# The B and C parameters of an S5 layer, loaded in pairs onto 128 partitions

## The chip, the cores and the metric

One core of a Trainium2 chip runs the whole model as one program. The metric is the time of the program on the device in microseconds (us). The kernel before took 1530.77 us in the median of 3 runs (1530.55 to 1533.98). The profiled execution took 1534.4 us, of which 1532.5 us are the profile's span.

The engines named here: PE does the matrix products, DVE and ACT the elementwise work, POOL some small things, SP issues nearly all DMA transfers, in its own program order. Each engine runs its instructions strictly in the order in which they were written.

## The reference, cut to what matters

Two layers work on 256 latent and 256 context tokens of width 2048, all in float32. Layer 0 multiplies the modulated input with a matrix of 2048x6144; beside attention heads it has a bidirectional S5 state-space group, whose parameters are discretized first:

```
h  = x  * (1 + sc) + sh          # sc, sh, gt = split(silu(c) @ ada_w + ada_b)
u  = h @ w_in[:, 4096:5120]      # 64 groups of 16 channels
lb = exp(a * dt);  f = (lb - 1) / a;  bb = f * b      # complex, 2 directions x 64 groups x 64 states (x 16)
state[t] = lb * state[t-1] + bb @ u[t];   y[t] = Re(c @ state[t])
```

`s5_b_re`, `s5_b_im`, `s5_c_re` and `s5_c_im` are the four arrays that this case is about: each has 2 x 64 x 1024 float32 values, 512 KB.

## The kernel before

**The stage.** The change lies in the first stage, which ends about 196 us after the span's start. Three streams meet in it on PE.

- The modulation. `ada_blocks` multiplies silu(c) with the first 4096 columns of `ada_w`: 8 blocks of 256 columns, 4 pieces each, so 32 groups of 8 matmuls `a<-adp,cst`. I count them from 1 to 32. Each group needs a pair of DMA loads into a tile `adp` (two times 512 KB); there are three such tiles (AHEAD = 3), so the load for group n+3 is issued only when group n is done. 33.6 MB come in this way.
- The modulated input. `h_blocks` transposes the tokens (`sb<-ident,xs`), block by block, and ACT and DVE make the two-part form `big_h`, `big_l`.
- The main products. `first` multiplies each block of the input with 11 (blocks 1 to 5) or 8 (blocks 6 to 8) column tiles of `w_in`. A float32 product is made of three passes (high times high, high times low, low times high), so the stage has 158 triples of `128x512` matmuls, 474 matmuls. The weights come as tiles `raw` of 384 to 512 KB, which ACT and DVE split into `hi` and `lo`.

**The S5 parameters.** `s5_params` is a generator that runs in the background of the same stage, from block 2 on. It loads each of the four arrays into a tile `nat` with the 64 groups on partitions 0 to 63 (line 764), and there is one such tile only. B is turned by 2 x 8 transposes per array, C by 2 x 16 small matmuls with the identity (both `sb<-ident,nat`), and ACT copies the result from the bank into the tile `cc`. Between B and C stand the powers of the discretized step (`cpow`, on DVE, into `pw`), the two copies of them into `pd_t` (ACT), and the six products of 128x1024 that make `bbar` from B (DVE). B's products use the tile `nat` as scratch (`tb`). C takes B's place in `cc`, and so comes after the last product.

**What sets the order.** Before the program is built, Python code (`Clock`) keeps an estimated time for every engine and for the DMA queue. After each triple of main matmuls `pump` asks which background generators are due by these estimates, and lets them write their next instructions. So every change of an instruction's estimated time, a load's above all, can move all that is written after it on every engine. On the chip nothing of these estimates is left but the order: PE waits at a group whose load has not landed, even if main products further down are ready.

Of the kernel before, what the change touches and what calls it, by code (L numbers as in the profile page):

```python
# [23 lines left out]
F32 = mybir.dt.float32  # L24
# [6 lines left out]
P = 128  # L31
# [10 lines left out]
G = 64  # L42
# [7 lines left out]
def dram(t, offset, ap):  # L50
    return bass.AP(tensor=t.tensor, offset=t.offset + offset, ap=ap)
# [197 lines left out]
def backbone(ctx: ExitStack, tc: tile.TileContext, A, out):  # L249
    nc = tc.nc  # L250
    clock = Clock()
    V, S, PE = Timed(nc.vector, "dve", clock), Timed(nc.scalar, "act", clock), Timed(nc.tensor, "pe", clock)
    GP, SY = Timed(nc.gpsimd, "gp", clock), Timed(nc.sync, "sp", clock)
# [3 lines left out]
    def pool(stack, name, bufs, **kw):  # L257
        pools.append(Pool(stack.enter_context(tc.tile_pool(name=name, bufs=bufs, **kw)), clock, bufs))
        return pools[-1]
# [20 lines left out]
    def hbank():  # L280
        return sbs[0].tile([P, 512], F32, name="sb")

    def vacant():

        while sbs[0].free("sb") > clock.now() + 0.05:
            clock.ready = sbs[0].free("sb") - pace["margin"]
            yield
# [7 lines left out]
    def act(o, i, f=AF.Copy, **kw):  # L295
        return S.activation(o, i, f, **kw)


    ident = const.tile([P, P], F32, name="ident")
# [183 lines left out]
    def aform(t0, n, nk=KT, k0=0):  # L483

        ps = mbank()
        for k in range(nk):
            if k % 8 == 0:
                wh, wl = ws.get()
            mm3(ps[:, :n], wh[:, k % 8, :], wl[:, k % 8, :], big_h[:, k0 + k, t0:t0 + n], big_l[:, k0 + k, t0:t0 + n],
                k == 0, k == nk - 1)  # L490
            used[0] = k
            pump()
        return ps
# [253 lines left out]
    def s5_params(sp, pp):  # L747
        tl, ts, ar, ai = (T5[n] for n in ("tl", "ts", "ar", "ai"))
        l8 = sp.tile([P, 2, 2, G], F32, name="l8")
        pd_t = sp.tile([P, 8, 2, G], F32, name="pd_t")  # L750
        bbar = sp.tile([P, 2, G + 1, 16], F32, name="bbar")
        cc = sp.tile([P, 2, G, 16], F32, name="cc")
        dcol = sp.tile([32, G], F32, name="dcol")
        zk = sp.tile([32, 16], F32, name="zk")
        T5.update(l8=l8, pd_t=pd_t, bbar=bbar, cc=cc, dcol=dcol, zk=zk)
        dn = pp.tile([G, 16], F32, name="dn")
        SY.dma_start(dn, dram(A["s5_d"], 0, [[16, G], [1, 16]]))
        bre, bim = cc[:, 0], cc[:, 1]
        dst = {"s5_b_re": bre, "s5_b_im": bim, "s5_c_re": cc[:, 0], "s5_c_im": cc[:, 1]}
        nat = {}  # L760

        def load_nat(nm):
            t = pp.tile([P, 2048], F32, name="nat")[:G]
            SY.dma_start(t.rearrange("g (k n) -> g k n", k=2),
                         dram(A[nm], 0, [[1024, G], [G * 1024, 2], [1, 1024]]))
            nat[nm] = t

        def params(nm):
            t = nat.pop(nm)
            for c8 in range(2):  # L770
                yield from vacant()
                p = hbank()
                for c_ in range(8):
                    c = c8 * 8 + c_
                    o = p[:, c_ * G:(c_ + 1) * G]
                    if "_b_" in nm:
                        PE.transpose(o, t[:, c::16], ident[:G, :G])
                    else:
                        for k in range(2):
                            PE.matmul(o[64 * k:64 * k + 64], t[:, k * 1024 + c * 64:k * 1024 + c * 64 + 64],  # L780
                                      ident[:G, :G], start=True, stop=True)
                act(dst[nm][:, :, c8 * 8:c8 * 8 + 8], p.rearrange("p (c g) -> p g c", c=8),
                    scale=-1.0 if nm == "s5_c_im" else 1.0)
                yield

        load_nat("s5_b_re")
        yield
        yield from vacant()
        pa = hbank()
        PE.transpose(pa[:16, :G], dn, ident[:G, :G])  # L790
        V.memset(dcol, 0.0)
        V.tensor_copy(dcol[:16], pa[:16, :G])
        V.memset(zk, 0.0)
        V.tensor_copy(zk[:16], ident[:16, :16])
        V.memset(bbar[:, :, G], 0.0)
        yield
        yield from params("s5_b_re")
        load_nat("s5_b_im")
        yield
        yield from params("s5_b_im")  # L800
        pw = pp.tile([P, 9, 2, G], F32, name="pw")
        V.memset(pw[:, 0, 0], 1.0)
        V.memset(pw[:, 0, 1], 0.0)
        V.tensor_mul(pw[:, 1, 0], tl("mag"), tl("cn"))
        V.tensor_mul(pw[:, 1, 1], tl("mag"), tl("sn"))
        den, nr, f = tl("t0"), tl("t1"), pp.tile([P, 2, G], F32, name="f")
        V.tensor_mul(den, ar, ar)
        V.tensor_mul(tl("t2"), ai, ai)
        V.tensor_add(den, den, tl("t2"))
        V.reciprocal(den, den)  # L810
        ni = pw[:, 1, 1]
        ts(nr, pw[:, 1, 0], -1.0, None, OP.add)
        V.tensor_mul(f[:, 0], nr, ar)
        V.tensor_mul(tl("t2"), ni, ai)
        V.tensor_add(f[:, 0], f[:, 0], tl("t2"))
        yield "dve"
        V.tensor_mul(f[:, 1], ni, ar)
        V.tensor_mul(tl("t2"), nr, ai)
        V.tensor_sub(f[:, 1], f[:, 1], tl("t2"))
        for s in range(2):  # L820
            V.tensor_mul(f[:, s], f[:, s], den)
        yield
        tp4 = pp.tile([P, 4, G], F32, name="tp4")

        def cpow(lo, cnt, by):

            s0 = lo - by
            xr, xi = pw[:, s0:s0 + cnt, 0], pw[:, s0:s0 + cnt, 1]
            yr = pw[:, by, 0][:, None, :].to_broadcast([P, cnt, G])
            yi = pw[:, by, 1][:, None, :].to_broadcast([P, cnt, G])  # L830
            t = tp4[:, :cnt]
            V.tensor_mul(pw[:, lo:lo + cnt, 0], xr, yr)
            V.tensor_mul(t, xi, yi)
            V.tensor_sub(pw[:, lo:lo + cnt, 0], pw[:, lo:lo + cnt, 0], t)
            V.tensor_mul(pw[:, lo:lo + cnt, 1], xr, yi)
            V.tensor_mul(t, xi, yr)
            V.tensor_add(pw[:, lo:lo + cnt, 1], pw[:, lo:lo + cnt, 1], t)

        cpow(2, 1, 1)
        yield "dve"  # L840
        cpow(3, 2, 2)
        yield "dve"
        cpow(5, 4, 4)
        yield "dve"
        for s in range(2):
            V.tensor_copy(l8[:, 0, s], pw[:, 8, 0])
        ts(l8[:, 1, 0], pw[:, 8, 1], -1.0, None)
        V.tensor_copy(l8[:, 1, 1], pw[:, 8, 1])
        act(pd_t[:64], pw[:64, 7::-1])
        act(pd_t[64:], pw[64:, :8])  # L850
        yield
        fr = f[:, 0, :, None].to_broadcast([P, G, 16])
        fi = f[:, 1, :, None].to_broadcast([P, G, 16])
        tb = pp.tile([P, 2048], F32, name="nat")[:, :1024].rearrange("p (g c) -> p g c", c=16)
        V.tensor_mul(bbar[:, 0, :G], bre, fr)
        yield "dve"
        V.tensor_mul(tb, bim, fi)
        yield "dve"
        V.tensor_sub(bbar[:, 0, :G], bbar[:, 0, :G], tb)
        yield "dve"  # L860
        V.tensor_mul(bbar[:, 1, :G], bim, fr)
        yield "dve"
        V.tensor_mul(tb, bre, fi)
        yield "dve"
        V.tensor_add(bbar[:, 1, :G], bbar[:, 1, :G], tb)
        load_nat("s5_c_re")
        yield
        yield from params("s5_c_re")
        load_nat("s5_c_im")
        yield  # L870
        yield from params("s5_c_im")
        yield

# [197 lines left out]
    pp = pool(pp5, name="pp5", bufs=1)  # L1071
# [304 lines left out]
    def hilo(o, ps, n=512, bufs=1):  # L1376
        h = att.tile([P, 512], F32R, name=o + "h", bufs=bufs)
        l = att.tile([P, 512], F32R, name=o + "l", bufs=bufs)
        act(h[:, :n], ps)
        V.tensor_sub(l[:, :n], ps, h[:, :n])  # L1380
        return h, l
# [113 lines left out]
    for h in range(NAH):  # L1495
# [13 lines left out]
        k = hilo("k", aform(0, NT))  # L1509
# [132 lines left out]
    t, st_ = layer0_half(1)  # L1642
# [75 lines left out]
    for hf in range(2):  # L1718
# [3 lines left out]
        for n in range(4):  # L1722
# [4 lines left out]
            else:  # L1727
                o = slice((n - 2) * 256, (n - 1) * 256)
# [71 lines left out]
    for hp in range(8):  # L1800
# [3 lines left out]
        r = rms(qx.rearrange("p t h d -> p (t h) d"))  # L1804
# [23 lines left out]
    with ExitStack() as es:  # L1828
# [5 lines left out]
        t = fp.tile([P, 2, D], F32, name="t1")  # L1834
        st_ = fp.tile([P, 2, 8, 6], F32, name="st1")
        mv = fp.tile([P, 2, 2], F32, name="mv1")
        nm = fp.tile([P, 1], F32, name="nm")
# [43 lines left out]
        for i in range(2):  # L1881
# [19 lines left out]
            if i == 1:  # L1901
                V.scalar_tensor_tensor(nm, mv[:, i, 0:1], -1.0, rs2, op0=OP.mult, op1=OP.mult)
                o, g, b = parts[3]
# [4 lines left out]
            for c in range(len(own) + 1):  # L1908
                if c < len(own):
                    o, g, b = own[c]  # L1910
                    V.scalar_tensor_tensor(o, o, mv[:, i, 0:1], g, op0=OP.subtract, op1=OP.mult)
                if c > 0:
                    o, g, b = own[c - 1]
# [46 lines left out]
```

## Time and profile before

| | us |
|---|---|
| median of 3 runs | 1530.77 |
| the profiled execution | 1534.4 |
| its span | 1532.5 |
| PE busy | 1478.4 |
| DVE busy | 982.8 |
| ACT busy | 641.7 |

PE is busy for 96% of the span, so a change is worth what it gives to or takes from PE's time without a break. The first stage is the only one in which DMA is as full as PE: the 16 DMA engines are busy throughout from 20 us to 110 us, with some 300 to 365 GB/s moved. A DMA share can stand a little above 1, as the records of transfers overlap.

To read the rows below: a timeline row has the start in us, the duration in us, the engine, line, operation, tiles out<-in, sizes and count, and in brackets the idle time of the engine just before it and what ended it. All operations go through one helper, so all have line L212; the tiles tell them apart. In the trace an fp32 matmul of the order stands as two, so a group of 8 shows as x16.

### The profile page before, as it was taken

To read this page: it belongs to the slowest core of one execution; us is meant where nothing else is said; L and a number is where in the kernel's file an instruction comes from. 1 tells how busy PE (TensorE), PEld (TensorE's weight loads), DVE (VectorE), ACT (ScalarE), POOL (GpSimd) and SP (SyncE) were. 2 spreads that over 40 slices of the span, in tenths; PEclk is the share of its full clock that TensorE was granted. 3 is DMA by queue.
4 is the path that set the end of the run, shared out by engine and by line. 5 is a ranking of instruction groups with operands and counts; after the bars stand their busy time and mean duration, and the time that the engine had idled before them with its cause. 6 is when DMAs were issued, how large, how long until landed. Compare 5 with 4: busy or idle time off the path is not lost.

```text
span 1532.5 us, 30530 instructions
## 1 busy us (share of the span) xinstructions
PE 1478.4 (96%) x12530; PEld 1283.4 (84%) x12530; DVE 982.8 (64%) x1721; ACT 641.7 (42%) x981; POOL 154.1 (10%) x308
## 2 busy tenths in 40 slices
PE   6998988999999999999999999999999999999996
PEld 3676777667789977888878999999899999999995
DVE  5356479988622688554447765665666666677597
ACT  2332244422355443433335533443454565665540
POOL 1000000000000033300000000100421211121021
PEclk8999999999999999999999999999999999999998
DMA  9998374676889577658877698886465445444684
GB/s 326 335 330 265 119 220 144 208 248 203 261 286 298 166 201 166 162 192 239 251 215 230 199 348 297 285 300 200 147 223 178 133 149 151 125 124 152 205 259 142
DMA packets 329919, 332.70 MB, mean 217 GB/s; under 512 B 40196, under 2 KB 287924, under 8 KB 329140
## 3 DMA queue, kind: packets, MB, share of 16 engines
q1 hardware_dynamic: 323540, 314.87, 65.8%
q0 software_dynamic: 6240, 15.88, 3.9%
q8 instruction: 98, 1.61, 0.4%
q14 instruction: 41, 0.34, 0.1%
HBM read 301.92 MB, written 24.54 MB: 213 GB/s over the span
## 4 chain that ended last, share of the span: by engine, by line
PE 79%; DVE 7%; DMA 7%; issue 4%; POOL 2%; SPq 1%; ACT 1%; DVEq 0%; POOLq 0%; ACTq 0%
PE m L212 59%; PE b L212 11%; PE a L212 6%; PE sb L212 4%; DVE dd L212 2%; DMA aw<-in_ada_w_dram 2%; DMA raw<-in_ev_w_in_dram 1%; DVE t L212 1%; SPq L212 1%; DVE lo L212 1%; DMA nat<-in_s_c_im_dram 1%; DMA gf<-in_ln_b_dram 1%; POOL gbr L212 1%; POOL rt L212 1%; DMA nat<-in_s_c_re_dram 1%
## 5 line engine op out<-in xcount | busy, mean ns | idle before, releaser
L212 ACT ACTIVATE hi<-raw 128x1024 fp32r<-128x1024 f32 (+1 forms) x253 | 265.2, 1050 | 319.2 <-PE m L212 166.5
L212 PE MATMUL m<-hi,big_h 128*128 128x256 f32 x1224 | 351.8, 287 | 0.1
L212 PE MATMUL m<-hi,big_l 128*128 128x256 f32 x1224 | 347.3, 284 | 0.0
L212 DVE TENSOR_TENSOR lo<-raw,hi 128x1024 fp32r<-128x1024 f32 (+1 forms) x214 | 257.2, 1209 | 110.9 <-issue 55.4
L212 PE MATMUL m<-lo,big_h 128*128 128x256 f32 x1152 | 326.9, 284 | 0.0
L212 PE MATMUL m<-big_h,hi 128*128 128x512 f32 (+1 forms) x848 | 319.6, 377 | 2.1 <-DVE acc L212 1.4
L212 PE MATMUL m<-big_l,hi 128*128 128x512 f32 (+1 forms) x848 | 309.3, 365 | 0.0
L212 PE MATMUL m<-big_h,lo 128*128 128x512 f32 (+1 forms) x832 | 304.6, 366 | 0.0
L212 PEld LDWEIGHTS m<-hi,big_h 128*128 128x128 f32 x1224 | 235.6, 192 | 7.3 <-issue 6.6
L212 PEld LDWEIGHTS m<-hi,big_l 128*128 128x128 f32 x1224 | 235.6, 193 | 0.2 <-DVE big_l L212 0.2
L212 PEld LDWEIGHTS m<-lo,big_h 128*128 128x128 f32 x1152 | 222.0, 193 | 0.1
L212 PEld LDWEIGHTS m<-big_h,hi 128*128 128x128 f32 x848 | 160.2, 189 | 39.9 <-issue 11.7
L212 PEld LDWEIGHTS m<-big_h,lo 128*128 128x128 f32 x832 | 157.1, 189 | 26.4
L212 PEld LDWEIGHTS m<-big_l,hi 128*128 128x128 f32 x848 | 160.5, 189 | 21.2
L212 PE MATMUL m<-lox,big_h 128*128 128x256 f32 x384 | 108.6, 283 | 0.0
L212 PE MATMUL m<-hix,big_h 128*128 128x256 f32 x312 | 89.1, 285 | 0.0
L212 PE MATMUL m<-hix,big_l 128*128 128x256 f32 x312 | 88.3, 283 | 0.0
L212 POOL DMA_DIRECT2D Yd<-ys x64 | 38.0, 600 | 407.7 <-DVE ys L212 407.0
L212 PEld LDWEIGHTS m<-lox,big_h 128*128 128x128 f32 x384 | 73.6, 192 | 0.3
L212 ACT ACTIVATE hix<-raw 128x1024 fp32r<-128x1024 f32 x45 | 47.5, 1056 | 49.9 <-PE m L212 16.9
L212 PE MATMUL a<-aw,cst 128*32 128x256 f32 x1024 | 65.4, 384 | 2.5 <-DMA aw<-in_ada_w_dram 2.4
L212 DVE TENSOR_TENSOR lox<-raw,hi 128x1024 fp32r<-128x1024 f32 x39 | 47.6, 1221 | 21.6 <-PE m L212 14.6
(383 smaller groups left out, 2192.9 us busy)
## 6 DMA issues: line engine op xcount, KB each, us to landing
aw<-in_ada_w_dram SPq DMA_DIRECT2D x128, 512.0 KB, 5.8
raw<-in_od_w_in_dram SPq DMA_DIRECT2D x96, 512.0 KB, 3.8
raw<-in_ev_w_in_dram SPq DMA_DIRECT2D x90, 512.0 KB, 5.0
adp<-in_ada_w_dram SPq DMA_DIRECT2D x64, 512.0 KB, 8.6
raw<-in_ev_w_out_dram SPq DMA_DIRECT2D x64, 512.0 KB, 6.1
raw<-in_od_w_out_dram SPq DMA_DIRECT2D x32, 512.0 KB, 4.9
ub<-Ud SPq DMA_DIRECT2D x32, 128.0 KB, 5.1
Sd<-sx SPq DMA_DIRECT2D x16, 256.0 KB, 6.5
```

The costliest lines, as they stand in the source:

```text
L212: r = f(*a, **kw)
```

## The change

- `load_nat` takes two names and loads the two arrays into one tile: the first on partitions 0 to 63, the second on partitions 64 to 127. They stay two DMAs of 512 KB each, now issued one behind the other. `params` transposes each from its half, with the identity of that half.
- `s5_b_im` is loaded together with `s5_b_re`, ahead of the first transposes; both C arrays are loaded together right behind B's transposes, ahead of the powers. Before, each of the last three loads was issued only when the array before it was done with.
- B's products no longer use a tile of the name `nat` as scratch, but the tile `pd_t`. The two ACT copies that fill `pd_t` with the powers have moved behind the last product.

```
-        def load_nat(nm):
-            t = pp.tile([P, 2048], F32, name="nat")[:G]
-            SY.dma_start(t.rearrange("g (k n) -> g k n", k=2),
-                         dram(A[nm], 0, [[1024, G], [G * 1024, 2], [1, 1024]]))
-            nat[nm] = t
+        def load_nat(*names):
+            t = pp.tile([P, 2048], F32, name="nat")
+            for r, nm in zip((0, G), names):
+                SY.dma_start(t[r:r + G].rearrange("g (k n) -> g k n", k=2),
+                             dram(A[nm], 0, [[1024, G], [G * 1024, 2], [1, 1024]]))
+                nat[nm] = t[r:r + G], ident[r:r + G, r:r + G]
...
-        load_nat("s5_b_re")
+        load_nat("s5_b_re", "s5_b_im")
...
         yield from params("s5_b_re")
-        load_nat("s5_b_im")
-        yield
         yield from params("s5_b_im")
+        load_nat("s5_c_re", "s5_c_im")
...
-        act(pd_t[:64], pw[:64, 7::-1])
-        act(pd_t[64:], pw[64:, :8])
...
-        tb = pp.tile([P, 2048], F32, name="nat")[:, :1024].rearrange("p (g c) -> p g c", c=16)
+        tb = pd_t.rearrange("p i s g -> p (i s g)").rearrange("p (g c) -> p g c", c=16)
...
-        load_nat("s5_c_re")
-        yield
+        yield
+        act(pd_t[:64], pw[:64, 7::-1])
+        act(pd_t[64:], pw[64:, :8])
         yield from params("s5_c_re")
-        load_nat("s5_c_im")
-        yield
         yield from params("s5_c_im")
```

The order moves with it on all engines of the first stage, and by little in the later ones. Two places matter below.

SP, the loads around groups 23 to 26. Before, no C load stands here; the first of them comes after the pair for group 28:

```order
L212 DMA raw_1004<-in_ev_w_in_dram 128x2x512
L212 DMA adp<-in_ada_w_dram 128x4x256 x2
L212 DMA raw_1081<-in_ev_w_in_dram 128x2x512
L212 DMA raw_1166<-in_ev_w_in_dram 128x2x384
L212 DMA adp<-in_ada_w_dram 128x4x256 x4
```

The first `adp` row is the pair for group 24, the second holds those for 25 and 26. The same place after the change, where the first `adp` row is the pair for group 23, the second that for 24, the last those for 25 and 26:

```order
L212 DMA adp<-in_ada_w_dram 128x4x256 x2
L212 DMA nat<-in_s_c_re_dram 64x2x1024
L212 DMA nat<-in_s_c_im_dram 64x2x1024
L212 DMA raw_1009<-in_ev_w_in_dram 128x2x384
L212 DMA adp<-in_ada_w_dram 128x4x256 x2
L212 DMA raw_1117<-in_ev_w_in_dram 128x2x512
L212 DMA adp<-in_ada_w_dram 128x4x256 x4
```

Both C loads now stand between the pairs for groups 23 and 24, and three `raw` loads have become two.

PE, the main products around groups 23 and 24 (`m<-big_h,hi` and its two companions are one triple). Before:

```order
L212 MATMUL m<-big_h,hi_928 128x512
L212 MATMUL m<-big_l,hi_928 128x512
L212 MATMUL m<-big_h,lo_998 128x512
L212 MATMUL a<-adp,cst 32x256 x16
L212 MATMUL m<-big_h,hi_928 128x512
L212 MATMUL m<-big_l,hi_928 128x512
```

After the change:

```order
L212 MATMUL a<-adp,cst 32x256 x8
L212 MATMUL m<-big_h,hi_771 128x512
L212 MATMUL m<-big_l,hi_771 128x512
L212 MATMUL m<-big_h,lo_845 128x512
L212 MATMUL m<-big_h,hi_771 128x512
L212 MATMUL m<-big_l,hi_771 128x512
L212 MATMUL m<-big_h,lo_845 128x512
L212 MATMUL a<-adp,cst 32x256 x8
```

Groups 23 and 24, which stood back to back behind 231 main matmuls, stand behind 183 and 189 now, with two triples between them; the tile numbers tell that the main products are one and a half weight pieces less far (`hi_771` is the last piece of block 3, `hi_928` a piece of block 4).

## Rows read from the trace of the kernel before

**Rows 1.** Chain that ended last, 0 to 200 us: start, duration, what.

```profile
128.66 7.75 DMA nat<-in_s_c_re_dram
...
143.49 11.79 DMA nat<-in_s_c_im_dram
...
196.20 0.22 DVE acc L212
```

**Rows 2.** Timeline of PE, 84 to 160 us.

```profile
85.16 1.07 PE L212 MATMUL a<-adp,cst 128*32 128x256 f32 x16
...
113.77 1.93 PE L212 MATMUL a<-adp,cst 128*32 128x256 f32 x32
...
121.04 1.07 PE L212 MATMUL a<-adp,cst 128*32 128x256 f32 x16
...
126.95 0.50 PE L212 MATMUL m<-big_h,hi 128*128 128x512 f32 x1 [1.42 <-DVE acc L212]
...
136.54 1.15 PE L212 MATMUL sb<-ident,nat 64*64 64x64 f32 x32 [2.67 <-DMA nat<-in_s_c_re_dram]
137.62 3.58 PE L212 MATMUL a<-adp,cst 128*32 128x256 f32 x32
...
155.42 1.15 PE L212 MATMUL sb<-ident,nat 64*64 64x64 f32 x32 [0.54 <-DMA nat<-in_s_c_im_dram]
```

**Rows 3.** Timeline of PE, two main matmuls with seven between them.

```profile
111.87 0.39 PE L212 MATMUL m<-big_l,hi 128*128 128x512 f32 x1
...
113.45 0.39 PE L212 MATMUL m<-big_h,lo 128*128 128x512 f32 x1
```

**Rows 4.** Windows: from:to, length, busy and (instructions) by engine, PEclk, DMA share, GB/s.

```profile
0.00:20.00 20.00, 10.15 (x78) 4.39 (x79) 13.53 (x89) 2.52 (x6) 3.98 (x12) 1.00 0.91 289
20.00:40.00 20.00, 17.16 (x94) 9.99 (x92) 7.58 (x14) 7.27 (x10) 0.00 (x0) 0.74 1.08 365
40.00:60.00 20.00, 19.73 (x150) 12.99 (x149) 4.67 (x8) 7.98 (x14) 0.00 (x0) 1.00 1.09 357
60.00:80.00 20.00, 20.00 (x139) 13.32 (x137) 10.56 (x20) 5.50 (x9) 0.00 (x0) 1.00 1.09 319
80.00:100.00 20.00, 20.00 (x144) 14.10 (x144) 7.99 (x12) 5.56 (x10) 0.00 (x0) 1.00 1.09 305
100.00:110.00 10.00, 10.00 (x74) 7.11 (x73) 6.91 (x28) 3.25 (x6) 0.00 (x0) 1.00 1.08 362
110.00:120.00 10.00, 10.00 (x78) 6.48 (x78) 9.64 (x26) 3.90 (x5) 0.00 (x0) 1.00 0.86 293
```

**Rows 5.** Windows of 4 us, the same columns.

```profile
60.00:64.00 4.00, 4.00 (x38) 2.44 (x40) 2.35 (x3) 1.02 (x2) 0.00 (x0) 1.00 1.10 297
64.00:68.00 4.00, 4.00 (x30) 2.94 (x23) 1.38 (x2) 1.97 (x3) 0.00 (x0) 1.00 1.08 211
68.00:72.00 4.00, 4.00 (x17) 2.74 (x16) 3.38 (x10) 0.00 (x0) 0.00 (x0) 1.00 1.09 349
...
88.00:92.00 4.00, 4.00 (x30) 2.63 (x29) 2.85 (x4) 1.61 (x3) 0.00 (x0) 1.00 1.11 214
92.00:96.00 4.00, 4.00 (x30) 2.59 (x29) 2.37 (x4) 0.00 (x0) 0.00 (x0) 1.00 1.08 238
...
136.00:140.00 4.00, 3.46 (x56) 2.23 (x60) 1.05 (x2) 0.60 (x1) 0.00 (x0) 0.70 0.41 133
```

**Rows 6.** Timeline of SP, 50 to 165 us: two of the four loads.

```profile
58.02 0.60 SPq L212 DMA_DIRECT2D nat<-in_s_b_re_dram  x1
...
82.87 1.87 SPq L212 DMA_DIRECT2D nat<-in_s_b_im_dram  x1
```

**Rows 7.** Instructions that touch tile nat: durations min/median/max in ns, first and last start.

```profile
L212 PE MATMUL sb<-ident,nat x160: 218/218/319, 73.4 to 159.0; 64*64 64x64 f32 x128, 64*128 64x64 f32 x32
L212 DVE TENSOR_TENSOR nat<-cc,f x2: 1217/1218/1219, 119.7 to 125.1; 128x1024 f32<-128x1024 f32 x2
```

**Rows 8.** Instructions that write tile pd_t, 0 to 200 us, the same columns.

```profile
L212 ACT ACTIVATE pd_t<-pw x2: 1057/1058/1060, 114.1 to 115.2; 64x1024 f32<-64x1024 f32 x2
```

More of the change, by code (lines that the diff above doesn't have):

```diff
@@ L760, in s5_params @@
         nat = {}
-        def load_nat(nm):
-            t = pp.tile([P, 2048], F32, name="nat")[:G]
-            SY.dma_start(t.rearrange("g (k n) -> g k n", k=2),
-                         dram(A[nm], 0, [[1024, G], [G * 1024, 2], [1, 1024]]))
-            nat[nm] = t
+        def load_nat(*names):
[4 more added lines that the diff above has]
+                nat[nm] = t[r:r + G], ident[r:r + G, r:r + G]
         def params(nm):
-            t = nat.pop(nm)
+            t, eye = nat.pop(nm)
             for c8 in range(2):
@@ L776, in params @@
                     if "_b_" in nm:
-                        PE.transpose(o, t[:, c::16], ident[:G, :G])
+                        PE.transpose(o, t[:, c::16], eye)
                     else:
@@ L780, in params @@
                             PE.matmul(o[64 * k:64 * k + 64], t[:, k * 1024 + c * 64:k * 1024 + c * 64 + 64],
-                                      ident[:G, :G], start=True, stop=True)
+                                      eye, start=True, stop=True)
                 act(dst[nm][:, :, c8 * 8:c8 * 8 + 8], p.rearrange("p (c g) -> p g c", c=8),
```

## The prediction

> **What bounds the kernel now.** I read the windows of the first 200 us first, then the timeline of PE, then SP's, then the chain of waits. PE is busy almost without a break from 40 us on [rows 4], so the stage that ends at 196.2 us [rows 1] is bound by PE. The reader is to see that DMA is as full there: its share is 1.08 or 1.09 from 20 us to 110 us, and only in 110 to 120 us does it fall, to 0.86 [rows 4]. So nothing can be loaded earlier without something else being loaded later. The chain of waits passes through the loads of C twice, with 7.75 and 11.79 us [rows 1], and invites one to count 19.5 us. But PE works on other things meanwhile: its timeline has the idle time, 2.67 us at c_re and 0.54 us at c_im [rows 2]. A third gap, 1.42 us, is a wait for DVE's sums [rows 2], among B's products. After the longest gap PE's clock stands at 0.70 in 136 to 140 us [rows 5] (the mean of its two levels, 2.4 and 1.2 GHz), and two groups of modulation matmuls take 3.58 us instead of 1.93 [rows 2].
>
> So at most 2.67 + 0.54 + 1.42 = 4.6 us are to be had from the waits, and 3.58 - 1.93 = 1.65 us more from the clock.
>
> **A load of one array costs more than its bytes.** Where b_re and b_im travel (issued at 58.0 and 82.9 us [rows 6]; those of C took 7.75 and 11.79 us to land [rows 1]), DMA moves 211 GB/s in 64 to 68 us, and 214 and 238 in 88 to 96 us, against 349 in 68 to 72 us, at the same share of 1.08 to 1.11 [rows 5]. The engines are occupied, but slow. Against 350 GB/s the first load loses (53 + 139) x 4 = 768 KB or 2.2 us, the second (136 + 112) x 4 = 992 KB or 2.8 us; I take 2.5 us. With its own 0.52 MB (1.5 us) a load into 64 partitions costs 4.0 us of the DMA stream.
>
> **The change part by part.** Removed are the waits for C: its loads are issued long before they are needed, so 2.67 and 0.54 us go. The 1.42 us I count as gone too, since B's products now stand elsewhere among the main products. I leave the 1.65 us of slow clock alone: it goes with this wait, but the waits found below can bring it back.
>
> Scratch and copies: the same two DVE instructions of 1.22 us write `pd_t` instead of `nat` [rows 7]. The two ACT copies of 1.06 us [rows 8] are the same, only later; queued behind them on ACT are a weight split and copies out of the banks, and if the products are late, PE's next transposes wait for those. I count 0, up to 2 us. The transposes from partitions 64 to 127 are as many and of the same shapes as now; none such is in the trace. Between no cost and a doubling of half of the 160 records (at the pace of 32 in 1.15 us [rows 2, 7], 80 x 36 ns = 2.9 us) I take 0, as the work per instruction is the same.
>
> Moved is what matters. In the order on SP b_im stands a whole block ahead of its old place, and both C loads stand between the pairs for groups 23 and 24, where before they came after group 28. In PE's order the groups come much earlier against the main products: 138 main matmuls stand ahead of group 18 where it was 150, 189 ahead of group 24 (231), 198 ahead of group 26 (246), 255 ahead of group 32 (324). The main matmuls follow each other every (113.45 - 111.87)/7 = 0.226 us [rows 3]. PE therefore comes to group 18 at 85.2 - 12 x 0.226 = 82.5 us, to group 24 at 114.8 - 42 x 0.226 = 105.3 us (it is the second half of the row at 113.77), and to group 26 at 121.0 - 48 x 0.226 = 110.2 us [rows 2], if it never waits. Behind PE's wait at a group all main products are queued, ready or not.
>
> Can DMA have the data there? SP's order has 38.75 MB up to and with the pair for group 26 before, and 38.88 MB now: the C loads came in and two weight pieces went behind. The windows give 20 x (289 + 365 + 357 + 319 + 305) + 10 x 362 = 36.3 MB up to 110 us [rows 4]; the 2.4 MB left take 8.3 us at 293 GB/s, so the pair lands at 118.3 us before, or a little later; it was used at 121.04, which is the upper bound. Now:
> - 0.13 MB more: +0.4 us.
> - The dip to 293 GB/s in 110 to 120 us came of loads that had to wait for PE's groups, which now come early. Filled to 350 it gives back 570 KB: -1.6 us.
> - Ahead of group 26 there are four loads into 64 partitions instead of two: +2 x 2.5 = +5.0 us, if each costs what one costs now.
>
> The pair lands at 118.3 + 3.8 = 122.1 us, or at 124.8 from the upper bound. PE wants it at 110.2, and so waits some 12 us in all, spread over groups 18 to 26.
>
> From there on PE is the bound again. After group 26 it has 48 main matmuls more to do than before, 48 x 0.226 = 10.8 us, and saves the three gaps, 4.6 us, all of which lay after 121 us. The stage's end thus moves by (landing - 121.0) + 10.8 - 4.6, which is landing minus 114.8. For 122.1 this is +7.3 us, for 124.8 +10.0 us. Group 32 does not decide: up to its pair SP has 47.1 MB instead of 48.7, and the emptied stretches such as 136 to 140 us at 133 GB/s [rows 5] fill up, so DMA is ahead of PE there. I take +7.2 us, by the measured byte count and not the upper bound.
>
> The later stages start from the end of this one, so the shift passes on whole; their order differs only in small exchanges, for which I allow 2 us to either side. Against the profiled execution of 1534.4 us (span 1532.5) this is 1541.6 us; that execution was 3.6 us above the median of the runs, 1530.8, and from the median I predict 1538 us.
>
> **The rivals.**
>
> *The pair travels side by side.* The second load of a pair writes the other half of the partitions. If both together ran at the 349 GB/s of full-width loads [rows 5], none of the four would lose the 2.5 us, the two of today included: the landing is 118.3 + 0.4 - 1.6 - 5.0 = 112.1 to 114.8 us, and the end moves by -2.7 to 0 us. The time is 1529.5 us. For it: the slow stretch looks like half of a full rate. Against it: DMA's share is above 1 in these stretches [rows 5], so no engine is free to take up the other load. Half of that effect gives 117.1 to 119.8 us, +2.3 to +5.0 us, and about 1534 us. No row of this trace shows two such loads at once. The Trainium skill (SBUF — State Buffer, "Can I just issue two DMAs to hit both halves?") speaks against this rival: it says that two concurrent transfers, one at partition 0 and one at 64, gained only 6% over one, since they serialize. By that the landing is near 122 us and the end near +7.
>
> *PE never waits; faster.* If DMA kept up with PE's new order, all that is left is the removed gaps and the clock: -4.6 - 1.65 = -6.3 us, 1524.5 us. It decides from the point at which 38.9 MB are in by 110.2 us. From 20 us (5.8 MB in) that is 33.1 MB in 90.2 us, 367 GB/s on average, against the 339 of 20 to 110 us now; only 20 to 40 us reached 365 [rows 4]. For it: the slow stretches pull today's mean down, and without them it would be near 350. Still short.
>
> *The change does nothing here.* If the new order's waits and the removed ones cancel, the landing is at 114.8 us; this lies within the first rival.
>
> *More goes wrong.* ACT blocked by the late copies (2 us), transposes from the upper half at double the cost (2.9 us) and the upper bound of the landing (+10) reach 1543 us and beyond.
>
> **How the numbers follow.** Serial loads, 1535.5 to 1543 us: 0.50, and beyond 0.02. Half side by side, around 1534: 0.20. Wholly side by side, around 1529.5: 0.14. No waits, 1524.5: 0.14. The range that holds the time 8 times in 10 reaches from 1528 to 1543, which leaves out most of the last case and the tail above; the likeliest case's own range is 1535.5 to 1543. A change of 0.3%, 4.6 us, is about what a measurement of this kernel can tell from none. Slower than 1535.4: the serial cases, 0.51. Faster than 1526.2: the last case and a little of the one before, 0.15. Between: 0.34.
>
> **What would show it.** Right: in the changed profile PE has idle time before modulation groups between 82 and 125 us, put down to `adp` loads, about 12 us in all, the longest behind the C loads near group 24; the group before which 198 main matmuls stand starts near 122 us; GB/s falls to 200 to 240 twice, for about twice as long as now; PE has no wait for `nat` after that; the stage ends near 203 us. Wrong: the windows with the pairs show 300 GB/s or more (side by side); PE is busy without a break up to 125 us, and the stage ends at 190 us (no waits); or the stage ends as said and the rest takes it back, which would be in the scan and attention stages after 200 us.

## The result, and the profile after

The changed kernel takes 1553.1 us in the median of 4 runs (1547.31 to 1555.58), the kernel before 1530.66 us (1527.84 to 1533.98) beside it: a ratio of 1.0136, interval [1.0104, 1.0168]. It is slower, as forecast, but by 22 us and not by 7, and the time lies beyond the range. The profiled execution took 1547.31 us (span 1545.5, against 1532.5), so the profiles show 13 us of it. It is the shortest of the four runs of the changed kernel, while the profiled execution of before, 1534.4 us, lies above all four of its runs.

| stretch, cut at the same main matmul in both | before, us | after, us | difference |
|---|---|---|---|
| start to the end of the first stage (matmul 473) | 195.8 | 200.8 | +5.0 |
| to matmul 2600 (787 us before) | 591.3 | 588.8 | -2.5 |
| to matmul 2660 (811 us before) | 23.5 | 35.0 | +11.5 |
| to the last matmul | 706.5 | 705.0 | -1.5 |
| tail to the end of the span | 15.4 | 16.0 | +0.6 |

The main matmuls are counted in the order of their start, from the timelines; there are 7488 in both. Two places hold the loss: the first stage and a stretch near 805 us. Of the 11.5 us there, 3.7 us is work that stood before matmul 2600 in the kernel before (one round of 32 modulation matmuls, x64 in the trace, 3.66 us a round), which more than accounts for the -2.5 us above it; the two rows together give +9.0 us.

**The first stage.** The windows of the changed kernel, with the columns of [rows 4]. The first three and 104 to 112 us are those in which the pairs travel:

```profile
60.00:64.00 4.00, 4.00 (x41) 2.40 (x43) 2.35 (x3) 0.96 (x2) 0.00 (x0) 1.00 1.11 299
64.00:68.00 4.00, 4.00 (x27) 2.99 (x20) 1.38 (x2) 1.70 (x3) 0.00 (x0) 1.00 1.02 200
68.00:72.00 4.00, 4.00 (x18) 3.01 (x18) 3.60 (x7) 0.27 (x1) 0.00 (x0) 1.00 1.10 264
...
80.00:84.00 4.00, 0.19 (x2) 0.20 (x2) 0.04 (x1) 1.33 (x2) 0.00 (x0) 1.00 1.09 356
84.00:88.00 4.00, 4.00 (x36) 2.14 (x39) 0.17 (x1) 0.93 (x2) 0.00 (x0) 0.59 1.09 359
...
92.00:96.00 4.00, 4.00 (x33) 2.49 (x32) 3.05 (x14) 1.34 (x3) 0.00 (x0) 1.00 0.71 227
...
104.00:108.00 4.00, 3.13 (x15) 2.30 (x16) 3.93 (x12) 0.16 (x1) 0.00 (x0) 1.00 1.07 238
108.00:112.00 4.00, 3.73 (x27) 2.04 (x26) 3.97 (x5) 1.18 (x3) 0.00 (x0) 1.00 1.04 259
```

Against 350 GB/s the B pair loses (51 + 150 + 86) x 4 = 1148 KB or 3.3 us, the C pair (112 + 91) x 4 = 812 KB or 2.3 us. A single load lost 2.2 and 2.8 us [rows 5]. So a pair loses about as much as one load, and not twice 2.5 us (2.3 us for each pair, by the same sum, in a second profile of this kernel). Between the pairs stands something else: PE is busy for 0.19 us of the 4 us from 80 to 84 us. The timeline of PE (idle time before an instruction and what ended it in brackets; one group of modulation matmuls is x16):

```profile
83.81 0.61 PE L212 MATMUL sb<-pick,arow 128*128 128x4 f32 x4 [3.95 <-ACT arow L212]
84.34 1.59 PE L212 MATMUL a<-adp,cst 128*32 128x256 f32 x16
...
105.66 0.50 PE L212 MATMUL m<-big_h,hi 128*128 128x512 f32 x1 [0.87 <-DVE acc L212]
...
112.45 0.50 PE L212 MATMUL m<-big_h,hi 128*128 128x512 f32 x1 [0.72 <-DVE acc L212]
...
114.59 1.06 PE L212 MATMUL a<-adp,cst 128*32 128x256 f32 x14 [0.63 <-DMA adp<-in_ada_w_dram]
...
118.91 1.06 PE L212 MATMUL a<-adp,cst 128*32 128x256 f32 x14 [0.67 <-DMA adp<-in_ada_w_dram]
...
121.91 1.06 PE L212 MATMUL a<-adp,cst 128*32 128x256 f32 x14 [0.51 <-DMA adp<-in_ada_w_dram]
```

The last three are what is left of groups 24, 25 and 26 after their first two records. They wait for their loads, as forecast, but 1.8 us in all; the longest wait is at the row vector `arow`, ahead of group 17. ACT makes it, and ACT stood behind a weight split (timeline of ACT):

```profile
82.42 1.06 ACT L212 ACTIVATE hi<-raw 128x1024 fp32r<-128x1024 f32 x1 [2.89 <-DMA raw<-in_ev_w_in_dram]
83.39 0.37 ACT L212 ACTIVATE arow<-a 128x256 f32<-128x256 f32 x1
```

In the kernel before, ACT made the same vector ahead of that split, and not behind it:

```profile
77.11 0.38 ACT L212 ACTIVATE arow<-a 128x256 f32<-128x256 f32 x1 [0.80 <-PE a L212]
79.20 1.06 ACT L212 ACTIVATE hi<-raw 128x1024 fp32r<-128x1024 f32 x1 [1.71 <-DMA raw<-in_ev_w_in_dram]
```

So two things came together: the `raw` of this split lands some 3 us later, and in ACT's new order `arow` has to wait for the split. Then a `raw` load holds ACT, ACT holds PE, and PE, held ahead of group 17, does nothing that would free an `adp` tile: the hole of 227 GB/s at 92 to 96 us follows. After the wait PE's clock is at half for a while (0.59 in 84 to 88 us). The four loads are issued in two pairs now (timeline of SP, the rows that answer to [rows 6]), and no instruction of PE waits for `nat` any more:

```profile
57.90 0.60 SPq L212 DMA_DIRECT2D nat<-in_s_b_re_dram  x1
58.54 0.61 SPq L212 DMA_DIRECT2D nat<-in_s_b_im_dram  x1
99.02 0.64 SPq L212 DMA_DIRECT2D nat<-in_s_c_re_dram  x1
99.70 0.61 SPq L212 DMA_DIRECT2D nat<-in_s_c_im_dram  x1
```

The stage ends 5 us later than in [rows 1] (timeline of DVE):

```profile
201.20 0.69 DVE L212 TENSOR_TENSOR acc<-acc,m 128x512 f32<-128x512 f32 x1 [0.67 <-PE m L212]
```

**Near 805 us.** Here, in the last of the attention heads of layer 0, a modulation of layer 1 has to be finished: a background generator, `ada_quad`, streams its weights (tiles `aw`) beside the heads, and the last head writes out what is left of it. The chain of waits of the kernel before (start, duration, what):

```profile
798.43 3.64 PE a L212 x64
...
802.74 0.66 PE a L212 x4
803.39 0.70 PE m L212 x3
```

And that of the changed kernel:

```profile
798.88 3.63 PE a L212 x64
...
803.86 9.28 DMA aw<-in_ada_w_dram
...
813.19 1.12 PE a L212 x8
...
814.99 1.12 PE a L212 x4
816.10 1.28 PE m L212 x3
```

A whole round of eight loads is issued only here (SP), and PE takes them one at a time, five of the eight steps with as much waiting as work, and the last two at half clock (PE, and the window of 812 to 816 us with PEclk at 0.50):

```profile
799.51 4.82 SPq L212 DMA_DIRECT2D aw<-in_ada_w_dram  x8
```

```profile
805.58 0.64 PE L212 MATMUL a<-aw,cst 128*32 128x256 f32 x8 [0.24 <-DMA aw<-in_ada_w_dram]
806.85 0.64 PE L212 MATMUL a<-aw,cst 128*32 128x256 f32 x8 [0.63 <-DMA aw<-in_ada_w_dram]
...
813.19 1.08 PE L212 MATMUL a<-aw,cst 128*32 128x256 f32 x8 [0.16 <-DMA aw<-in_ada_w_dram]
```

```profile
812.00:816.00 4.00, 3.12 (x21) 1.37 (x22) 0.00 (x0) 1.54 (x2) 0.00 (x0) 0.50 0.17 31
```

Why is a round left? The first load of the stream on SP, before and now:

```profile
668.09 0.50 SPq L212 DMA_DIRECT2D aw<-in_ada_w_dram  x1
```

```profile
703.54 0.50 SPq L212 DMA_DIRECT2D aw<-in_ada_w_dram  x1
```

The code says when it may start: at the top of each head (counted from 0), `if adab is None and "done" in s5_have:`, that is, once the planner has written out all of S5's output. In the kernel before that is so at the top of head 3. In the changed kernel S5 is later in the plan: its last output matmuls (`sb<-ub,tt`) stand behind 2145 main matmuls and no longer behind 2130. The question at head 3 is just missed, and the stream starts a head later, with one head fewer to run beside. All this is settled when the order is written, by the planner's estimates; no delay on the chip can move it.

### The profile page after: what moved, and what is told of

The parts are those of the page before. It is cut to its first block, busy times and chain, and to the rows that moved or that the text cites. A ratio compares the mean times of both kernels' runs of the same rounds, so it can differ in the third digit from the quotient of the medians.

```text
span 1545.5 us, 30540 instructions
## 1 busy us (share of the span) xinstructions
PE 1483.0 (96%) x12530; PEld 1282.6 (83%) x12530; DVE 982.5 (64%) x1721; ACT 641.1 (41%) x981; POOL 153.8 (10%) x308
## 4 chain that ended last, share of the span: by engine, by line
PE 75%; DMA 8%; DVE 8%; issue 4%; POOL 2%; SPq 1%; ACT 1%; DVEq 0%; ACTq 0%; POOLq 0%
PE m L212 57%; PE b L212 9%; PE a L212 5%; PE sb L212 3%; DMA raw<-in_ev_w_in_dram 2%; DVE dd L212 2%; SPq L212 1%; DMA aw<-in_ada_w_dram 1%; DMA adp<-in_ada_w_dram 1%; DVE t L212 1%; DMA tt<-kp 1%; DVE lo L212 1%; DMA gf<-in_ln_b_dram 1%; POOL gbr L212 1%; POOL rt L212 1%
## 5 line engine op out<-in xcount | busy, mean ns | idle before, releaser
L212 ACT ACTIVATE hi<-raw 128x1024 fp32r<-128x1024 f32 (+1 forms) x253 | 265.2, 1050 | 310.7 <-PE m L212 176.2
L212 PE MATMUL m<-hi,big_h 128*128 128x256 f32 x1224 | 351.0, 287 | 0.0
L212 PE MATMUL m<-hi,big_l 128*128 128x256 f32 x1224 | 347.1, 284 | 0.0
L212 DVE TENSOR_TENSOR lo<-raw,hi 128x1024 fp32r<-128x1024 f32 (+1 forms) x214 | 257.4, 1209 | 133.8 <-issue 68.5
L212 PE MATMUL m<-lo,big_h 128*128 128x256 f32 x1152 | 326.6, 283 | 0.0
L212 PE MATMUL m<-big_h,hi 128*128 128x512 f32 (+1 forms) x848 | 319.7, 377 | 2.6 <-DVE acc L212 1.9
L212 PE MATMUL m<-big_l,hi 128*128 128x512 f32 (+1 forms) x848 | 309.6, 365 | 0.0
L212 PE MATMUL m<-big_h,lo 128*128 128x512 f32 (+1 forms) x832 | 304.8, 366 | 0.0
L212 PEld LDWEIGHTS m<-hi,big_h 128*128 128x128 f32 x1224 | 235.2, 192 | 6.5 <-issue 6.0
L212 PEld LDWEIGHTS m<-hi,big_l 128*128 128x128 f32 x1224 | 235.3, 192 | 0.2 <-DVE big_l L212 0.2
L212 PEld LDWEIGHTS m<-lo,big_h 128*128 128x128 f32 x1152 | 221.6, 192 | 0.1
L212 PEld LDWEIGHTS m<-big_h,hi 128*128 128x128 f32 x848 | 160.3, 189 | 40.7 <-issue 12.1
L212 PEld LDWEIGHTS m<-big_h,lo 128*128 128x128 f32 x832 | 157.2, 189 | 26.6
L212 PEld LDWEIGHTS m<-big_l,hi 128*128 128x128 f32 x848 | 160.6, 189 | 21.2
L212 PE MATMUL m<-lox,big_h 128*128 128x256 f32 x384 | 108.6, 283 | 0.0
L212 PE MATMUL m<-hix,big_h 128*128 128x256 f32 x312 | 89.2, 286 | 0.0
L212 PE MATMUL m<-hix,big_l 128*128 128x256 f32 x312 | 88.3, 283 | 0.0
L212 POOL DMA_DIRECT2D Yd<-ys x64 | 37.7, 595 | 418.4 <-DVE ys L212 417.7
L212 PEld LDWEIGHTS m<-lox,big_h 128*128 128x128 f32 x384 | 73.6, 192 | 0.3
L212 PE MATMUL a<-aw,cst 128*32 128x256 f32 x1024 | 68.0, 392 | 4.5 <-DMA aw<-in_ada_w_dram 4.5
L212 ACT ACTIVATE hix<-raw 128x1024 fp32r<-128x1024 f32 x45 | 47.5, 1056 | 56.7 <-DMA raw<-in_od_w_out_dram 20.9
L212 PEld LDWEIGHTS m<-hix,big_h 128*128 128x128 f32 x312 | 59.8, 192 | 0.5 <-issue 0.4
```

What stands on the lines that cost most here:

```text
L212: r = f(*a, **kw)
```

## The experiments

The theory: two mechanisms, the longer first stage (5 to 8 us) and the late start of the stream (some 11 us). The rivals: all of it is the first stage and is passed on; or the loads into half of the partitions cost the time. Each kernel was compared with the kernel before in the same batch. There were three batches (the first four runs below, the next four, the last three), and the median of the kernel before was 1533.0, 1533.2 and 1532.1 us in them.

**The changed kernel again.**

> The changed kernel once more, unaltered, to see where the runs near 1555 us differ from the profiled one of 1547 us. Theory 1 (two places: the first stage ends 5 us later, and 8 us go near 805 us, where a modulation stream that began one attention head later is waited for): the first stage ends at 201 to 203 us again, the wait near 805 us is there again, and a longer run is longer at that second place, since nothing else hangs on a load that was issued just before. Rival (the first stage is the one that varies, since it is the one that DMA bounds): in a run near 1555 us it ends at 207 to 210 us.

No edit. Measured: 1550.6 us (1545.67 to 1555.81), 1.0118 [1.0094, 1.0142]. The stage ends at 202.0 us, and the stretch of matmuls 2600 to 2660 takes 35.0 us again. What the two profiles show is the kernel's and not one execution's. Both are of short runs, though (1547.31 and 1545.67 us), so what a run near 1555 us loses in addition, and where, is not seen. Over the six runs the time rises as the mean granted clock falls (0.990 to 0.983, about 1.6 us for each 0.001), and single runs lie up to 10 us apart.

**The late start alone, in the kernel before.**

```
-        if adab is None and "done" in s5_have:
+        if adab is None and "done" in s5_have and h >= 4:
```

> The kernel before with one condition more: the modulation stream of layer 1 (ada_quad(1, 1)) starts at attention head 4 and no longer at head 3, as it does in the changed kernel. The first stage is word for word that of before. Theory 1: the last round of 8 loads is waited for near 800 us, with 8 to 9 us of PE time; 1539 to 1545 us. Rival (the later stages only shift and the loss is made in the first stage): 1531 us, within 2 us.

Measured: 1545.83 us, 1.0084 [1.0062, 1.0107]. One condition, with the first stage as it was, costs 12.8 us, a little more than expected. PE's timeline near the end of the heads:

```profile
794.50 0.64 PE L212 MATMUL a<-aw,cst 128*32 128x256 f32 x8 [0.93 <-DMA aw<-in_ada_w_dram]
799.36 1.08 PE L212 MATMUL a<-aw,cst 128*32 128x256 f32 x8 [4.21 <-DMA aw<-in_ada_w_dram]
```

The stretch from 2600 to 2660 takes 37.8 us instead of 23.5. The mechanism near 805 us is shown, and with it that it needs nothing of the S5 loads. (Its first stage, the same instructions as before, ended at 192.42 us and not 196.20: so far do two executions of one order differ.)

**The changed kernel with the early start.**

```
     for h in range(NAH):
+        if h == 3:
+            force(s5g)
```

> The changed kernel, but at attention head 3 the S5 work is written out to its end first, so that the modulation stream can start at head 3 as it did before. Theory 1: the wait near 805 us is gone, 8 to 14 us less than the changed kernel, 1539 to 1545 us, less what PE waits for S5 at head 3. Rival: as slow as the changed kernel, 1547 to 1556 us.

Measured: 1542.23 us, 1.0063 [1.0044, 1.0082], 8.4 us less than the unaltered change in the same batch. SP's first load of the stream and PE's last round:

```profile
676.44 0.50 SPq L212 DMA_DIRECT2D aw<-in_ada_w_dram  x1
```

```profile
806.35 3.66 PE L212 MATMUL a<-aw,cst 128*32 128x256 f32 x64
810.87 0.60 PE L212 MATMUL a<-ident,aw 128*128 128x128 f32 x4
```

No wait for `aw` is left and the stretch takes 22.7 us. With the two runs above this makes a square: the late start costs 12.8 us in the kernel before and 8.4 us in the changed one, and 9.2 us of the change's loss remain without it. In this run's profile the first stage ends at 203.46 us, 7.3 us after that of before, and matmul 2660 is still 7.2 us late, so up to there the shift is passed on whole, as the forecast had it. This profile is of the longest of the six runs (1549.22 us, clock 0.984), and loses another 6.7 us behind matmul 2660. That the 9.2 us of the medians are the first stage's is therefore likely, but not shown: kernels further down lose 5 to 10 us with a stage that ends in time.

**Full-width loads in the kernel before.**

```
-            t = pp.tile([P, 2048], F32, name="nat")[:G]
-            SY.dma_start(t.rearrange("g (k n) -> g k n", k=2),
-                         dram(A[nm], 0, [[1024, G], [G * 1024, 2], [1, 1024]]))
...
+            t = pp.tile([P, 2048], F32, name="nat")
+            for r, nm in zip((0, 1024), names):
+                SY.dma_start(t[:, r:r + 1024], dram(A[nm], 0, [[1024, P], [1, 1024]]))
...
+                        PE.matmul(o[h], t[h, c::16] if "_b_" in nm else t[h, c * 64:c * 64 + 64],
+                                  ident[h, h], start=True, stop=True)
```

> The kernel before, with each of the four S5 arrays loaded onto all 128 partitions in one transfer (direction and group on the partitions, 4 KB each), and B turned by the same small matmuls as C; places of the loads as before. Theory (a load into 64 partitions costs 2.5 us of the DMA stream over its bytes): GB/s no longer falls to 211 to 238 where B travels but stays at 340 or more; PE hardly waited for DMA there, so the first stage ends 0 to 3 us earlier; 1528 to 1531 us. Rival (the dips come of something else, such as the order of the requests): the dips stay, time unchanged.

Each array goes onto 128 partitions, and both halves are turned by small matmuls. Measured: 1531.63 us, 0.9996 [0.9986, 1.0007]. The windows that answer to the first five of [rows 5]:

```profile
60.00:64.00 4.00, 4.00 (x37) 2.41 (x39) 2.34 (x3) 1.01 (x2) 0.00 (x0) 1.00 1.07 389
64.00:68.00 4.00, 4.00 (x27) 2.99 (x20) 1.37 (x2) 1.97 (x3) 0.00 (x0) 1.00 1.09 354
68.00:72.00 4.00, 4.00 (x18) 2.62 (x16) 3.53 (x10) 0.00 (x0) 0.00 (x0) 1.00 1.08 363
...
88.00:92.00 4.00, 4.00 (x30) 2.86 (x29) 2.84 (x4) 2.09 (x3) 0.00 (x0) 1.00 0.90 300
92.00:96.00 4.00, 4.00 (x27) 2.76 (x19) 1.39 (x3) 0.00 (x0) 0.00 (x0) 1.00 0.90 286
```

354 GB/s stands where it was 211: the dip belongs to the layout on 64 partitions. In 88 to 96 us, where it was 214 and 238, it is 300 and 286, below the 340 expected; there the stream is no longer full (0.90 instead of 1.08 to 1.11). And yet the time does not move, and the stage ends at 197.20 us, no earlier than before: the kernel before has no time to win there, since PE is busy throughout.

**The pairs one by one.** First only B's pair (C's loads, copies and scratch as before), then only C's pair, early and with the scratch moved (B's loads as before). In both the stream starts at head 3. The edits are against the changed kernel, and of the first only the loads of C are shown in part.

```
         load_nat("s5_b_re", "s5_b_im")
...
-        load_nat("s5_c_re", "s5_c_im")
...
+        load_nat("s5_c_re")
+        yield
...
```

> The kernel before with B alone in a pair; C is loaded in its two old places, with the scratch in nat as before. Its PE order has the modulation groups as far forward as the changed kernel (183 main matmuls ahead of group 24, where before has 231 and the changed kernel 189), and the modulation stream of layer 1 starts at head 3 as before. Theory 1 (the first stage's loss is made by B's pair through the order of PE, the rest by the late start at head 4): PE waits between 80 and 125 us, the first stage ends 5 to 9 us late, there is no wait near 800 us; 1537 to 1543 us. Rival (C's pair ahead of group 24 is what delays the first stage): the stage ends within 2 us of before; 1530 to 1534 us.

```
-        load_nat("s5_b_re", "s5_b_im")
+        load_nat("s5_b_re")
...
+        load_nat("s5_b_im")
+        yield
```

> The changed kernel, but B's two arrays one after the other as before; C in a pair ahead of the powers, the scratch in pd_t. PE's order has groups 18 to 24 where before has them and 258 main matmuls ahead of group 26 (246), so the data of C's pair is there in time. Theory 1: PE waits for neither C nor modulation loads, the first stage ends 3 to 5 us earlier than before, the stream starts at head 3; 1526 to 1530 us. Rival (C's pair delays the first stage): 1533 to 1540 us.

Measured: B's pair alone 1552.78 us, 1.0116 [1.0093, 1.0139]; C's pair alone 1534.95 us, 1.0004 [0.9987, 1.0021]. Both times missed the expectation. B's pair alone has the long wait behind ACT, and its stage ends at 204.63 us (PE and DVE, from two timelines):

```profile
82.78 0.61 PE L212 MATMUL sb<-pick,arow 128*128 128x4 f32 x4 [3.16 <-ACT arow L212]
```

```profile
204.63 0.69 DVE L212 TENSOR_TENSOR acc<-acc,m 128x512 f32<-128x512 f32 x1 [0.67 <-PE m L212]
```

C's pair alone has no such wait, only 1.2 us for `adp` at group 25, and ends the stage at 190.65 us:

```profile
190.65 0.69 DVE L212 TENSOR_TENSOR acc<-acc,m 128x512 f32<-128x512 f32 x1 [0.67 <-PE m L212]
```

So the harm in the first stage comes with B's pair and the order that the planner makes with it: `b_im` stands a block ahead of its old place, the `raw` that ACT needs comes later, and here too `arow` stands behind the split on ACT (82.36 us, behind 81.40), where in C's pair alone it is ahead of it as before (77.09 us, ahead of 78.84). C's early loads, the moved scratch and the late copies of `pd_t` do none there. The second kernel's stage ends 5.5 us ahead of [rows 1], but only 1.8 us ahead of the other profile of the first stage of before (192.42 us), and its median shows no gain. The first lost some 8 us after its stage in the profile, with no late round; 3.2 of these are a new wait of PE for DVE (`ev`) at 223.9 us. The rest stays open.

**The change with full-width loads**, early start at head 3, by its own order:

```
-            for r, nm in zip((0, G), names):
-                SY.dma_start(t[r:r + G].rearrange("g (k n) -> g k n", k=2), ...
+            for r, nm in zip((0, 1024), names):
+                SY.dma_start(t[:, r:r + 1024], dram(A[nm], 0, [[1024, P], [1, 1024]]))
```

> The changed kernel, with each array on all 128 partitions in one transfer (direction and group on the partitions), two arrays side by side in one tile, B turned by small matmuls as C is. PE's order has 147 main matmuls ahead of group 18 and 231 ahead of group 24, near before's, and the stream starts at head 3. Theory 1: no dips below 300 GB/s where B and C travel, no PE waits for C or modulation loads of over 1 us, the first stage ends 2 to 6 us earlier than before; 1526 to 1531 us. Rival (two arrays loaded together cost the stage its time, whatever the layout): 5 us or more later than before, 1536 us or above.

Measured: 1538.96 us, 1.0027 [1.0011, 1.0044]. The stage ends at 194.86 us, and between 60 and 200 us PE waits only for DVE, 0.33 and 0.71 us, as the theory had it. That end is 1.3 us earlier than in [rows 1], less than two executions of one order differ by, and the time is not lower but 5.7 us higher: missed.

**The change with a denser stream.** The planned distance between two loads of the stream halved, the start still at head 4:

```
-            adab = background(ada_quad(1, 1, 1024, ap3, 8, 8, 2.0))
+            adab = background(ada_quad(1, 1, 1024, ap3, 8, 8, 1.0))
```

> The changed kernel with one number altered: the modulation stream of layer 1 paces its loads 1 us apart in the plan and not 2. It still starts at head 4. Theory 1 (the stream is a round short when it is forced): its four rounds are done by the time of the last head, the wait of 11 us near 805 us is gone or shrinks to under 3 us; 1539 to 1543 us. Rival (the start at head 4 costs by what it displaces, not by the unfinished round): 1548 to 1553 us.

Measured: 1549.63 us, 1.0093 [1.0068, 1.0118], within the rival's range. The stretch near 805 us takes 24.6 us again, with 2.0 us of wait for `aw` left. But from the end of the first stage to matmul 2660 it is 621.3 us, instead of 623.8 in the changed kernel and 614.8 in that before: with the round back ahead of matmul 2600, 2.5 us are won and not 10. Of what took it back, 3.2 us are waits of PE for S5's `tt` between 620 and 700 us; the rest is not settled. The profile is of the longest of the six runs (1555.39 us, clock 0.983).

**Another order of the first stage.** The planner's rate for DMA, which sets only the order, lowered from 360 GB/s for the first stage: in the changed kernel to 320, in the kernel before to 320, in the changed kernel to 300 (`bw` is 360e3 again from the stage's end on; the added line makes L212 into L213).

```
-        busy = max(words * 4 / 360e3, 0.18)
+        busy = max(words * 4 / self.bw, 0.18)
```

> The changed kernel, but its planner's estimate for DMA is 320 instead of 360 GB/s in the first stage. Everything else is computed as before. 144, 210, 237 and 306 main matmuls now stand ahead of groups 18, 24, 26 and 32, instead of 138, 189, 198 and 255, and the background stream of weights starts at head 3. Theory 1 (PE asked for groups whose data was not there, and the late start of the stream made the rest of the loss): the first stage ends at 194 to 199 us instead of 201 to 202, the stretch near 805 us takes 23 to 24 us again instead of 35, and the time is 1530 to 1536 us. Rival (the pairs cost DMA time that no order gives back): the stage ends at 201 us or later and the time is 1540 to 1546 us, as with the forced start at head 3 alone.

> The kernel before, with the planner's estimate for DMA at 320 instead of 360 GB/s in the first stage, and nothing else changed. Theory 1: the order in the first stage before was already close to what DMA delivers, so this gains little, 1527 to 1532 us. Rival (a lower rate helps any version): 1520 to 1526 us, and then what the runs with the changed kernel gain by it is no answer to the change.

> The changed kernel with the planner's estimate for DMA at 300 GB/s in the first stage: 156, 240, 261 and 351 main matmuls ahead of groups 18, 24, 26 and 32, so more than in the kernel before; the background stream starts at head 3. Theory 1: PE waits for no group any more; main products run out earlier and the last groups stand close together, so the stage ends at 190 to 197 us, the time is 1527 to 1534 us. Rival (the pairs cost DMA time that no order gives back): the stage ends at 201 us or later, the time is 1540 us or more.

Measured: 1542.04 us, 1.0055 [1.0036, 1.0074]; 1541.38 us, 1.0050 [1.0030, 1.0070]; 1537.15 us, 1.0033 [1.0014, 1.0051]. All three times lie above what the theory said. The ends of the stage in this order, each from DVE's timeline of its kernel:

```profile
193.87 0.69 DVE L213 TENSOR_TENSOR acc<-acc,m 128x512 f32<-128x512 f32 x1 [0.67 <-PE m L213]
```

```profile
196.08 0.69 DVE L213 TENSOR_TENSOR acc<-acc,m 128x512 f32<-128x512 f32 x1 [0.67 <-PE m L213]
```

```profile
194.76 0.69 DVE L213 TENSOR_TENSOR acc<-acc,m 128x512 f32<-128x512 f32 x1 [0.67 <-PE m L213]
```

With both pairs in it, the stage can end some 8 us sooner than in the changed kernel (first and third: 194.3 us in the mean, against 202.7 for the changed kernel's own order), and PE has no wait for `adp` in either: the stage was lost to the order, not to the bytes. In the first of them `arow` stands behind the weight split on ACT as well, but the split starts at 78.91 us and PE does not wait. The stretch near 805 us takes 20.7, 23.5 and 21.1 us. But the times are 5 to 10 us above the kernel before, for the kernel before itself too, whose stage ends as early as ever. Nothing of S5 was touched there: this new order alone costs 0.5%. Part of it goes between the end of the first stage and matmul 2600, which takes 593.8, 594.9 and 595.0 us in the three profiles and 591.3 before. Why it goes there I have not pinned down; in the profile of the second, PE is at half clock for 6.8 us from 284 us on (not so in the profile of before), and its waits for DVE and ACT between 200 and 340 us sum to 13.3 us instead of 10.1. No version beats the kernel before.

## Why the prediction was wrong

**What held.** The direction; that PE asks for its groups before the data is there; group 26, forecast for 122.1 us, which begins at 120.8 us and goes on at 121.91 us when its second load is there (in the second profile it begins at 122.69 us and waits no more); no wait for `nat` afterwards; PE without a break from 125 to 196 us. The end of the stage was to move by 7.2 us. The four profiles with the changed stage's order end at 201.2, 202.0, 203.5 and 204.3 us, the two with that of before at 196.2 and 192.4 us: 8.4 us between the means. The three other profiles of the changed order have the same long wait behind ACT, of 2.9 to 3.3 us.

**The step that failed:** "The later stages start from the end of this one, so the shift passes on whole; their order differs only in small exchanges, for which I allow 2 us to either side." What was wrong is the second half: the later order differs by more than small exchanges (nor does it move "by little", as the section on the change has it). In the new plan the end of S5 stands 15 main matmuls later, the question at the top of head 3 is missed, and the stream of 32 loads starts a head later. In place of the 2 us allowed, an unfinished round of eight loads cost 9.0 us net in the profiles (the rows of +11.5 and -2.5 us), 12.8 us when the late start was forced upon the kernel before, and 8.4 us came back when the changed kernel was made to start early. With that the change takes 1542.2 us, 4 us over the forecast and inside its range. Where the stream's first load stands among the heads could have been looked up in the two orders without a run: the forecast read the order only where the change was made.

**Right for partly wrong reasons.** Two terms of the first stage were mis-sized and cancelled. Two more half-width loads were to cost +5.0 us of the stream; the pairs lost 3.3 and 2.3 us, and the singles 2.2 and 2.8, so the second load of a pair costs next to nothing beyond its bytes: four loads lost 5.6 us where two lost 5.0. On the loads that is the rival's half measure ("half of that effect"); wholly side by side they would have lost nothing, and the windows would show 300 GB/s or more. The Trainium skill (SBUF — State Buffer, "Can I just issue two DMAs to hit both halves?"), which speaks of 6% gained, is not borne out by these windows: where it would have the loss nearly double, it stayed about the same, though here both loads ran inside a stream that was full of others. In place of that came a wait that I had not looked for, 3.95 us behind ACT and `raw` at 83.8 us, with a hole in DMA at 92 to 96 us (227 GB/s) after it. The forecast had 12 us of waits on `adp`; they were 1.8 us, and 7.2 us of idle PE in all between 80 and 125 us (37.80 of 45 us busy). That group 26 came at the forecast time is luck to that extent.

**What stays open.** The medians differ by 22 us, and by 17.6 us when the change was run again; the profiles differ by 13. The ten runs of the changed kernel have mean clocks of 0.983 to 0.990, 0.986 on average, those of before 0.985 to 0.992 with a mean of 0.989; the two profiles, at 0.987 and 0.986, have no such difference. Within each of the three batches, the runs of the kernel before take 0.6 to 1.8 us more for each 0.001 less. By that, an estimate of 2 to 5 us of the medians' difference goes with the clock and cannot be in the profiles. In the rows, half clock follows the waits (84 to 88 us, and 812 to 816 us), so fewer waits and a faster clock go together; that the clock is a cause of its own was not tested. Nor is it settled why four other kernels without the late round, with the stage's end no later than 196.1 us, have medians from 5 to 10 us above that of before (the fifth, C's pair alone, can't be told from it).

## What to carry to other kernels

Where a plan starts background work on a question asked at fixed points ("is that done yet?"), a shift of a few instructions in the plan can cost a whole step: look up in both orders where each such stream starts, not only the place that was edited. In an order written out beforehand, ask for each load that moves forward which load it pushes back, and who stands behind that one: here it was a weight piece, and PE stood behind ACT. Look up as well what changed places on the engines between: here a small row vector had moved behind the work on that piece. And before a gain or a loss of half a percent is put down to a change, run a version that only reorders: here such a version lost as much.

## What the hardware showed that was not expected

- A load of 512 KB into 64 partitions slows a full DMA stream to between 211 and 238 GB/s for 4 to 8 us at an unchanged share of 1.08 to 1.11; in the windows where the same bytes go onto 128 partitions into a full stream, it is 354 to 389 GB/s. Two such loads, one to each half and issued 0.6 to 0.7 us apart, lose 2.3 to 3.3 us against 350 GB/s, one alone 2.2 to 2.8 us.
- Steps of four modulation matmuls (x8 in the trace) that each wait for a load of their own cost twice: some 0.63 us of waiting for 0.64 us of work, five times in a row, and then 1.08 us for the same work at half clock (PEclk 0.50 in 812 to 816 us).
